# Column groups for a small projection, a later norm and earlier last-block preparations in a one-core decoder layer

## The chip, the core and the metric

The kernel runs on one core of a Trainium2 chip. The metric is the device time of one execution in microseconds, lower is better. The kernel before takes 1133.27 us, the median of 3 runs from 1133.16 to 1133.73. The engines are named as the profile names them: PE (TensorE), DVE (VectorE), ACT (ScalarE), POOL (GpSimd) and SP (SyncE, which issues most DMAs).

## What is computed

One decoder layer over 1088 tokens: a prompt of 1024 and 8 samples of 8 tokens. Three token mixers share one input projection; then comes a squared-ReLU MLP of width 4096. All is float32.

```python
h = rmsnorm(x, g1)
proj = h @ w_in            # 2816 columns of mixers A, B, C, and 8 columns dt_raw
...
dt = jax.nn.softplus(dt_raw + dt_bias)
y, ssm_new = ssd(xs, dt, A, Bm, Cm, ssm_prev)
yc = rmsnorm(y * jax.nn.silu(z), ssm_norm)
x = x + jnp.concatenate([ya, yb, yc], axis=-1) @ w_out
f = jnp.square(jax.nn.relu(rmsnorm(x, g2) @ w_ff1))
x = x + f @ w_ff2          # then the final norm
```

The norm of a token is a factor `rstd` that multiplies its projected columns afterwards, so the projections can start before it is known. `dt_raw` has only 8 columns.

## The kernel before

Tokens lie along the free axis, features along 128 partitions; x is 8 tiles (`xts[k]`) of 128 x 1088. Products are made from float32 pairs: every operand is split into a rounded high part and the rest (low part), in float32r, and a product is hi·hi + lo·hi + hi·lo, in three chunks of 364, 364 and 360 tokens (`CH`).

**Start.** The loop over k (from line 240) makes for each tile the high part of x times g1 (line 248 on DVE for the first three, line 246 on ACT for the others), the low part (line 251, DVE), the square of the tile before, in place (`square`, line 234, ACT), and from the fourth tile on adds a square to the sum `ss` (`add_square`, line 238, DVE). `w_split` casts a weight tile to its high part on ACT (line 100) and subtracts on DVE (line 101). The first gemm group (lines 327 to 338) runs over k and makes the first projection (lines 330 and 334) and the 8 dt columns (line 337): the dt weights are split in place into a tile of 32 columns (8 high, 8 low, 16 zeros, lines 203 to 207 and 254), so that one product with the high and one with the low part of x does, into 32 partitions, in three chunks. The second projection is a `gemm` over chunks (lines 131 to 133); after its first chunk stands `rms_scale` (line 172 on PE, then lines 173 to 183 on ACT and DVE), which makes `rstd` out of `ss`. Its chunks are evacuated times `rstd` (line 286), the first projection and dt are multiplied afterwards (lines 351 and 353), and `conv_c` follows for both: a start on ACT (line 300), three multiply-adds each on DVE (line 303), a SiLU (line 305), and small copies of the buffer's edges on POOL (lines 296 and 297). The buffers `cb` are two, so the third projection is evacuated into one that a `conv_c` has released. PSUM slots for the projections (`gp`) are three. `dt_tokens` (lines 373 and 375) turns dt to tokens by partition, by products between the chunks of the third projection.

**Last block.** The MLP goes in 8 blocks; in each, `ff1` and `ff2` make their products by seven weight combinations of four quarters (11, 12, 21, 22) of a weight block. `wsums` makes sums of quarters (lines 989 to 991), `prep` splits a combination (line 101, or line 908 into `wl` tiles for two of the last), `load_q` loads a quarter of the next half-block on SP (line 979), `operand` splits an activation form (lines 907 to 911; forms by line 937, which also adds products into x). In the last block `ff1` has products `pos` 0 to 6 in the order (1, 2, 6, 7, 5, 3, 4), and `ff2_last` goes through a list of units (position, row tile), each 12 products of 272 columns. A product group takes a PSUM bank; line 1189 is an ACT copy that frees two of them.

The order on each engine is fixed when the program is built. It follows the order of the code, but what is ready goes ahead of what is not; the tail from `last_products` on is in an order written out by hand. Each engine works its queue strictly in that order.

Of the kernel before, what the change touches and what calls it, by code (L numbers as in the profile page):

```python
# [15 lines left out]
P = 128  # L16
D = 1024
# [54 lines left out]
def body(nc, tc, I, O):  # L72
# [130 lines left out]
    wdt = sml.tile([P, KT, 32], F32R, name="wdt")  # L203
    wd = C("wdt").rearrange("p (k m) -> p k m", m=8)
    zz = sml.tile([P, KT, 16], F32, name="zz")
    G.memset(zz, 0.0)
    V.tensor_copy(out=wdt[:, :, 16:32], in_=zz)
# [31 lines left out]

    for k in range(KT):  # L240
        xt = xts[k]
        b = big[:, k * 2 * T:(k + 1) * 2 * T].rearrange("p (h t) -> p h t", h=2)
        g = C("g1")[:, k:k + 1]
        for a, e in (((0, 364), (364, T)) if k == 0 else ((0, T),)):
            if k > 2:
                S.activation(out=b[:, 0, a:e], in_=xt[:, a:e], func=AF.Identity, scale=g)
            else:
                V.tensor_scalar(out=b[:, 0, a:e], in0=xt[:, a:e], scalar1=g, scalar2=None, op0=ALU.mult)
        if k == 0:
            w_split(0)  # L250
        V.scalar_tensor_tensor(out=b[:, 1], in0=xt[:, :T], scalar=g, in1=b[:, 0].bitcast(F32),
                               op0=ALU.mult, op1=ALU.subtract)
        if k == 0:
            V.tensor_copy(out=wdt[:, :, 0:8], in_=wd)
            V.tensor_tensor(out=wdt[:, :, 8:16], in0=wd, in1=wdt[:, :, 0:8].bitcast(F32),
                            op=ALU.subtract)
        if k:
            square(k - 1)
        if k > 2:
            add_square(k - 2)  # L260
        xg.append(b)
    w_split(1)
    square(KT - 1)
    add_square(KT - 2)
    add_square(KT - 1)
# [59 lines left out]
    psd = [ap.tile([P, 512], F32, name="aps", tag="a") for _ in CH]  # L325
    w0 = next_w()
    for k in range(KT):
        for h in range(2):
            for ps, (c0, n) in zip(ps0, CH):
                PE.matmul(ps[:, :n], w0[:, 0, k * P:(k + 1) * P], xg[k][:, h, c0:c0 + n],  # L330
                          start=k == 0 and h == 0, stop=k == KT - 1 and h == 1)
            if h == 0:
                for ps, (c0, n) in zip(ps0, CH):
                    PE.matmul(ps[:, :n], w0[:, 1, k * P:(k + 1) * P], xg[k][:, 0, c0:c0 + n],
                              start=False, stop=False)
            for ps, (c0, n) in zip(psd, CH):
                PE.matmul(ps[:32, :n], wdt[:, k], xg[k][:, h, c0:c0 + n],  # L337
                          start=k == 0 and h == 0, stop=k == KT - 1 and h == 1)
# [4 lines left out]
    dtT = tmpp.tile([P, T], F32, name="dtT", tag="t")[:32]  # L343
    for ps, (c0, n) in zip(psd, CH):
        S.copy(out=dtT[:, c0:c0 + n], in_=ps[:32, :n])
    buf5 = new_buf(3, C("sst")[:, 5 * 24:6 * 24])
    gemm(next_w(), xg, range(KT), lambda c, ps: evac_pad(c, ps, buf5, 3),
         first=ap.tile([P, 512], F32, name="aps", tag="a"), hooks=[lambda: rms_scale(aslots(), catp, "yb", ss, rstd, D, False)])
# [4 lines left out]
    V.tensor_tensor(out=dtT, in0=dtT, in1=rstd[:32], op=ALU.mult)  # L353
# [13 lines left out]
    def dt_tokens(cs):  # L367
        if not dpv:
            dps = ap.tile([P, 512], F32, name="aps", tag="a")
            dpv.append(dps[:, :72].rearrange("p (c h) -> p c h", h=8))  # L370
        for c in cs:
            if c < NC:
                PE.matmul(dpv[0][:, c], dtT[:, c * L:(c + 1) * L], C("eye2")[:32], start=True, stop=True)
            else:
                PE.matmul(dpv[0][:TS, NC], dtT[:, SEQ:T], C("eye2")[:32], start=True, stop=True)
# [605 lines left out]
    def wsums(hb):  # L981
        if (hb, "s1") in raw:
            return
        a11, a21, a22 = (raw[hb, q] for q in ("11", "21", "22"))
        s1 = raw[hb, "s1"] = wrp.tile([P, 1024], F32, name="ws", tag="wr")
        raw[hb, "s2"] = a11
        if hb == 0:
            raw[hb, "s2"] = qtile("ws")[:, :1024]
        V.tensor_tensor(out=s1, in0=a21, in1=a22, op=ALU.add)
        V.tensor_tensor(out=a21, in0=a21, in1=a11, op=ALU.add)  # L990
        V.tensor_tensor(out=raw[hb, "s2"], in0=a11, in1=s1, op=ALU.add)
# [7 lines left out]
    def prep(n):  # L999
# [20 lines left out]
        if pos == 3:  # L1020
            load_q(hb + 1, "11")
            load_q(hb + 1, "21")
        if j == 4:
            load_q(hb + 1, "22")
        elif j == (6 if 0 < hb < 2 * NFB - 1 else 3):
            wsum4(hb)
            load_q(hb + 1, "12")
# [66 lines left out]
    def ff1(i):  # L1094
# [31 lines left out]
        for pos, j in enumerate(ords):  # L1126
# [33 lines left out]
            elif j == 6:  # L1160
                if i:
                    copy_out("12", ps)
                else:
# [9 lines left out]
            elif j == 3:  # L1173
                if i:
                    add_in("12", ps)
                    relu2("12", 1.0)
                    if i == NFB - 1:
                        operand(i, f, 0)
# [22 lines left out]
            if i == NFB - 1:  # L1201
                if pos == 4:
                    f["op22"] = fviews(x % 3 * XS)
                    split_f(f["op22"], f["22"], slice(0, NH), 1.0)
                elif pos == 5:
                    wsums(2 * NFB - 1)
                    prep(LAST2 + 4)
                elif pos == 6:
                    prep(LAST2 + 3)
# [27 lines left out]
    def ff2_operand(f, j, dst):  # L1237
        src = form(j, f["11"], f["12"], f.get("21"), f["22"], op)
# [64 lines left out]
    def ff2_last(f):  # L1303
# [15 lines left out]
        units = [(0, 0), (0, 1), (0, 2), (1, 0), (0, 3), (1, 1), (2, 0), (1, 2), (2, 1), (1, 3), (3, 0), (2, 2),  # L1319
# [281 lines left out]
```

## Time and profile before

| | |
|---|---|
| median of 3 runs | 1133.27 us |
| profiled execution, its own time | 1133.37 us |
| its span, first to last instruction | 1131.6 us |
| PE busy | 1118.3 us |
| DVE busy | 836.4 us |
| ACT busy | 498.3 us |
| POOL busy | 62.3 us |
| granted PE clock, mean | 0.997 of full |

Busy time is the union of an engine's instruction times. Matmuls are pipelined and their ends are modelled, so the distance between two starts says more than a duration. An idle engine costs something only where the chain that ended last passes through it.

### The profile page before, as it was taken

The numbers are of one execution on the slowest core, as the hardware profiler recorded it, in microseconds if no ns is written. First come the engines' busy times: TensorE is split into PE (matmuls) and PEld (weight loads), VectorE is DVE, ScalarE is ACT, GpSimd is POOL, SyncE is SP. The second block draws the span as 40 slices with busy tenths as digits, with TensorE's granted clock in tenths as the row PEclk, the third lists the DMA queues.
The fourth block names the chain that finished last, engine by engine and source line by source line (L and its number), as shares of the span: only waits on it lengthen the run. The fifth ranks groups of instructions, "written<-read, shape, count | busy, mean of one in ns | idle before, by whom it ended". The sixth has DMA issues, their size and how long they took to land.

```text
span 1131.6 us, 19854 instructions
## 1 busy us (share of the span) xinstructions
PE 1118.3 (99%) x8482; PEld 1099.0 (97%) x8482; DVE 836.4 (74%) x1108; ACT 498.3 (44%) x660; POOL 62.3 (6%) x94
## 2 busy tenths in 40 slices
PE   8999999999999999999999999999999999999996
PEld 6999999999999999999999999999999999999996
DVE  8875587965655476989697497497596596599596
ACT  6545273423553334753342442443443442533544
POOL 1410021110000000000000000000000000000016
PEclk9999999999999999999999999999999999999998
DMA  6112233321137253692853953953953943954404
GB/s 258 52 50 69 60 113 104 113 69 53 34 99 272 84 223 123 281 394 79 311 197 114 391 198 131 387 187 142 384 190 140 385 182 152 376 175 159 195 1 159
DMA packets 34776, 200.43 MB, mean 177 GB/s; under 512 B 4736, under 2 KB 7680, under 8 KB 27776
## 3 DMA queue, kind: packets, MB, share of 16 engines
q1 hardware_dynamic: 32592, 196.30, 46.8%
q10 hardware_dynamic: 2096, 2.85, 0.7%
q8 instruction: 67, 1.10, 0.4%
q14 instruction: 21, 0.17, 0.0%
HBM read 175.58 MB, written 22.77 MB: 175 GB/s over the span
## 4 chain that ended last, share of the span: by engine, by line
PE 94%; DVE 4%; DMA 1%; issue 0%; ACT 0%; POOL 0%; SPq 0%; POOLq 0%; ACTq 0%
PE ps L1035 19%; PE ps L1034 19%; PE ps L1036 18%; PE gps L131 10%; PE gps L132 10%; PE gps L133 10%; PE aps L565 1%; DVE x L937 1%; PE aps L569 1%; DVE whl L101 1%; DMA xt<-xT 1%; PE gps L330 1%; PE aps L337 0%; DVE xq L902 0%; DVE big L908 0%
## 5 line engine op out<-in xcount | busy, mean ns | idle before, releaser
L1034 PE MATMUL ps<-big,whl 128*128 128x272 f32 x1312 | 377.6, 288 | 0.2 <-DVE f L1116 0.2
L1035 PE MATMUL ps<-big,whl 128*128 128x272 f32 x1312 | 377.6, 288 | 0.0
L1036 PE MATMUL ps<-big,whl 128*128 128x272 f32 x1312 | 376.9, 287 | 0.0
L1034 PEld LDWEIGHTS ps<-big,whl 128*128 128x128 f32 x1312 | 247.1, 188 | 0.6 <-DVE f L1116 0.5
L1035 PEld LDWEIGHTS ps<-big,whl 128*128 128x128 f32 x1312 | 247.1, 188 | 0.0
L1036 PEld LDWEIGHTS ps<-big,whl 128*128 128x128 f32 x1312 | 246.8, 188 | 0.0
L131 PE MATMUL gps<-big,whl 128*128 128x360 f32 (+2 forms) x752 | 240.0, 319 | 0.0
L132 PE MATMUL gps<-big,whl 128*128 128x360 f32 (+2 forms) x752 | 236.6, 315 | 0.3 <-DVE whl L101 0.3
L133 PE MATMUL gps<-big,whl 128*128 128x360 f32 (+2 forms) x752 | 236.0, 314 | 0.0
L100 ACT CAST whl<-wq 128x1024 fp32r<-128x1024 f32 x92 | 96.5, 1051 | 226.7 <-PE ps L1036 131.3
L101 DVE TENSOR_TENSOR whl<-wq,whl 128x1024 fp32r<-128x1024 f32 x92 | 112.5, 1222 | 55.8 <-ACT whl L100 55.6
L131 PEld LDWEIGHTS gps<-big,whl 128*128 128x128 f32 x752 | 141.5, 188 | 0.9 <-ACT big L778 0.2
L132 PEld LDWEIGHTS gps<-big,whl 128*128 128x128 f32 x752 | 141.4, 188 | 0.9 <-DVE whl L101 0.5
L133 PEld LDWEIGHTS gps<-big,whl 128*128 128x128 f32 x752 | 141.3, 188 | 0.0
L937 DVE TENSOR_TENSOR x<-x,ps 128x544 f32<-128x544 f32 x188 | 130.6, 716 | 6.7 <-PE ps L1036 5.7
L1036 PE MATMUL ps<-fo,whl 128*128 128x272 f32 x416 | 119.6, 288 | 0.2 <-DVE fo L911 0.2
L1035 PE MATMUL ps<-fo,whl 128*128 128x272 f32 x416 | 119.3, 287 | 0.3 <-DVE whl L101 0.3
L1034 PE MATMUL ps<-fo,whl 128*128 128x272 f32 x416 | 119.4, 287 | 0.0
L100 ACT CAST whl<-wst 128x1024 fp32r<-128x1024 f32 (+2 forms) x39 | 40.0, 1026 | 133.2 <-PE gps L133 84.2
L1036 PEld LDWEIGHTS ps<-fo,whl 128*128 128x128 f32 x416 | 78.2, 188 | 0.7 <-DVE fo L911 0.7
L1035 PEld LDWEIGHTS ps<-fo,whl 128*128 128x128 f32 x416 | 78.2, 188 | 0.5 <-DVE whl L101 0.5
L1034 PEld LDWEIGHTS ps<-fo,whl 128*128 128x128 f32 x416 | 78.4, 188 | 0.1
(325 smaller groups left out, 1406.1 us busy)
## 6 DMA issues: line engine op xcount, KB each, us to landing
big<-xcd SPq DMA_DIRECT2D x47, 2176.0 KB, 9.9
wq<-w SPq DMA_DIRECT2D x66, 512.0 KB, 4.5
xcd<-big SPq DMA_DIRECT2D x7, 2176.0 KB, 8.6
wst<-w_in SPq DMA_DIRECT2D x21, 512.0 KB, 3.6
wst<-w_out SPq DMA_DIRECT2D x16, 512.0 KB, 3.6
x<-xT SPq DMA_DIRECT2D x8, 544.0 KB, 5.4
dec<-scr SPq DMA_DIRECT2D x8, 512.0 KB, 3.8
xt<-xT SPq DMA_DIRECT2D x7, 544.0 KB, 8.8
```

Of the source, the lines that this page charges most:

```text
L100: S.copy(out=w[:, 0, a:b], in_=st[:, a:b])
L101: V.tensor_tensor(out=w[:, 1, a:b], in0=st[:, a:b], in1=w[:, 0, a:b].bitcast(F32), op=ALU.subtract)
L131: PE.matmul(ps[:, :n], hi, xh, start=start, stop=False)
L132: PE.matmul(ps[:, :n], lo, xh, start=False, stop=False)
L133: PE.matmul(ps[:, :n], hi, xl, start=False, stop=stop)
L330: PE.matmul(ps[:, :n], w0[:, 0, k * P:(k + 1) * P], xg[k][:, h, c0:c0 + n], start=k == 0 and h == 0, stop=k == KT - 1 and h == 1)
L565: PE.matmul(yps[hh * HD:(hh + 1) * HD, i * L:(i + 1) * L], w[:, h * HD:(h + 1) * HD], m[:, h], start=i == 0 and n == 0, stop=n == len(term ...
L569: PE.matmul(sps[:, g * 256:(g + 1) * 256], bt[:, g * P:(g + 1) * P], xw[:, g * 256:(g + 1) * 256], start=True, stop=True)
L937: V.tensor_tensor(out=out, in0=a, in1=b, op=o)
L1034: PE.matmul(o, hi, xh, start=start and k == 0, stop=False, skip_group_check=True)
L1035: PE.matmul(o, lo, xh, start=False, stop=False, skip_group_check=True)
L1036: PE.matmul(o, hi, xl, start=False, stop=k == ks - 1, skip_group_check=True)
```

## The change

In the start: the dt weights are multiplied by g1 once and kept in plain float32, with 24 columns of zeros behind the 8. `dt_products(k)` multiplies them with the raw tile `xts[k]` as soon as it is loaded, in four groups of 256 prompt tokens, each into its own 32 partitions of one PSUM tile, and two groups of 32 sample tokens beside them. These stand in the code ahead of each tile's split; the 48 dt products in the first gemm group go. All additions of squares stand behind the loop and the second weight split. The norm (`rms_scale`) stands after the second chunk of the second projection instead of the first, and the first chunk's evacuation is held until then. dt is multiplied by `rstd` in six pieces, before the first projection is, and `dt_tokens` reads it from four partition groups, with one more product.

In the last block: for the last half-block quarter 22 is loaded before 12 instead of after it; `wsums` is made in two parts, the first two sums after `pos` 3; the split of combination 4 (`LAST2 + 3`) stands after `pos` 4 instead of 6; the first operand's split stands two products earlier; and in `ff2_last` unit (0, 3) stands before (1, 0).

```diff
@@ -200 @@
-    wdt = sml.tile([P, KT, 32], F32R, name="wdt")
-    wd = C("wdt").rearrange("p (k m) -> p k m", m=8)
-    zz = sml.tile([P, KT, 16], F32, name="zz")
-    G.memset(zz, 0.0)
-    V.tensor_copy(out=wdt[:, :, 16:32], in_=zz)
+    wdt = sml.tile([P, KT, 32], F32, name="wdt")
+    G.memset(wdt, 0.0)
@@ -237 @@
+    V.tensor_tensor(out=wdt[:, :, 0:8], in0=C("wdt").rearrange("p (k m) -> p k m", m=8),
+                    in1=C("g1").unsqueeze(2).broadcast_to([P, KT, 8]), op=ALU.mult)
+    psd = ap.tile([P, 512], F32, name="aps", tag="a")
+    DTQ = SEQ // 4
+
+    def dt_products(k):
+        parts = [(j, 0, DTQ, j * DTQ) for j in range(4)] + [(j, DTQ, 32, SEQ + 32 * j) for j in range(2)]
+        for j, o, n, t in parts:
+            PE.matmul(psd[32 * j:32 * j + 32, o:o + n], wdt[:, k], xts[k][:, t:t + n],
+                      start=k == 0 and o == 0, stop=k == KT - 1, skip_group_check=True)
+
     for k in range(KT):
         xt = xts[k]
+        dt_products(k)
...
-        if k == 0:
-            V.tensor_copy(out=wdt[:, :, 0:8], in_=wd)
-            V.tensor_tensor(out=wdt[:, :, 8:16], in0=wd, in1=wdt[:, :, 0:8].bitcast(F32),
-                            op=ALU.subtract)
         if k:
             square(k - 1)
-        if k > 2:
-            add_square(k - 2)
         xg.append(b)
     w_split(1)
     square(KT - 1)
-    add_square(KT - 2)
-    add_square(KT - 1)
+    for k in range(KT):
+        add_square(k)
@@ -333 @@
-            for ps, (c0, n) in zip(psd, CH):
-                PE.matmul(ps[:32, :n], wdt[:, k], xg[k][:, h, c0:c0 + n],
-                          start=k == 0 and h == 0, stop=k == KT - 1 and h == 1)
...
-    dtT = tmpp.tile([P, T], F32, name="dtT", tag="t")[:32]
-    for ps, (c0, n) in zip(psd, CH):
-        S.copy(out=dtT[:, c0:c0 + n], in_=ps[:32, :n])
+    dtT = tmpp.tile([P, T], F32, name="dtT", tag="t")[:, :DTQ + 32]
+    S.copy(out=dtT[:, :DTQ], in_=psd[:, :DTQ])
+    S.copy(out=dtT[:64, DTQ:], in_=psd[:64, DTQ:DTQ + 32])
...
-    gemm(next_w(), xg, range(KT), lambda c, ps: evac_pad(c, ps, buf5, 3),
-         first=ap.tile([P, 512], F32, name="aps", tag="a"), hooks=[lambda: rms_scale(aslots(), catp, "yb", ss, rstd, D, False)])
+    held = []
+
+    def evac_late(c, ps):
+        held.append((c, ps))
+        while c and held:
+            evac_pad(*held.pop(0), buf5, 3)
+
+    gemm(next_w(), xg, range(KT), evac_late, first=ap.tile([P, 512], F32, name="aps", tag="a"),
+         hooks=[lambda: None, lambda: rms_scale(aslots(), catp, "yb", ss, rstd, D, False)])
+    for j in range(4):
+        r = slice(32 * j, 32 * j + 32)
+        V.tensor_tensor(out=dtT[r, :DTQ], in0=dtT[r, :DTQ], in1=rstd[r, j * DTQ:(j + 1) * DTQ], op=ALU.mult)
+        if j < 2:
+            V.tensor_tensor(out=dtT[r, DTQ:], in0=dtT[r, DTQ:], in1=rstd[r, SEQ + 32 * j:SEQ + 32 * j + 32],
+                            op=ALU.mult)
...
-    V.tensor_tensor(out=dtT, in0=dtT, in1=rstd[:32], op=ALU.mult)
@@ -1020 @@
+        first, second = ("22", "12") if hb == 2 * NFB - 2 else ("12", "22")
         if j == 4:
-            load_q(hb + 1, "22")
+            load_q(hb + 1, second)
         elif j == (6 if 0 < hb < 2 * NFB - 1 else 3):
             wsum4(hb)
-            load_q(hb + 1, "12")
+            load_q(hb + 1, first)
@@ -1160 @@
                 if i:
                     copy_out("12", ps)
+                    if i == NFB - 1:
+                        operand(i, f, 0)
...
                     if i == NFB - 1:
-                        operand(i, f, 0)
                         operand(i, f, 1)
@@ -1202 @@
                 if pos == 4:
                     f["op22"] = fviews(x % 3 * XS)
                     split_f(f["op22"], f["22"], slice(0, NH), 1.0)
+                    prep(LAST2 + 3)
+                elif pos == 3:
+                    wsums(2 * NFB - 1, False)
                 elif pos == 5:
                     wsums(2 * NFB - 1)
                     prep(LAST2 + 4)
-                elif pos == 6:
-                    prep(LAST2 + 3)
@@ -1316 @@
-        units = [(0, 0), (0, 1), (0, 2), (1, 0), (0, 3), (1, 1), (2, 0), (1, 2), (2, 1), (1, 3), (3, 0), (2, 2),
+        units = [(0, 0), (0, 1), (0, 2), (0, 3), (1, 0), (1, 1), (2, 0), (1, 2), (2, 1), (1, 3), (3, 0), (2, 2),
```

## Rows read from the trace of the kernel before

**Rows 1.** The page, part 1: busy time, share of the span, instructions.

```profile
PE 1118.3 (99%) x8482; PEld 1099.0 (97%) x8482; DVE 836.4 (74%) x1108; ACT 498.3 (44%) x660; POOL 62.3 (6%) x94
```

**Rows 2.** Table by stretches: stretch; us, busy per engine (instructions); PEclk, DMA, GB/s.

```profile
38.00:56.00 18.00, 18.00 (x112) 17.23 (x111) 17.63 (x25) 7.79 (x7) 11.60 (x10) 1.00 0.10 30
60.00:1050.00 990.00, 989.46 (x7563) 979.21 (x7562) 726.49 (x949) 420.83 (x549) 24.50 (x48) 1.00 0.50 185
1075.50:1097.00 21.50, 21.50 (x174) 21.50 (x174) 21.50 (x27) 8.16 (x11) 0.00 (x0) 1.00 0.01 2
```

**Rows 3.** Timeline of PE, start: start, length, instruction, count, [idle before <-releaser].

```profile
4.49 0.77 PE L337 MATMUL aps<-big,wdt 128*32 128x364 f32 x1
...
27.53 0.33 PE L131 MATMUL aps<-big,whl 128*128 128x364 f32 x1
...
31.52 1.99 PE L172 MATMUL aps<-ss,cp 128*128 128x364 f32 x6
...
55.98 0.43 PE L131 MATMUL gps<-big,whl 128*128 128x364 f32 x1
```

**Rows 4.** Chain that ended last: start, length to the next step, what.

```profile
31.68 1.83 PE aps L172 x6
...
56.05 0.36 PE gps L131
56.42 0.17 PE gps L132
...
158.82 1.90 PE aps L565 x32
```

**Rows 5.** Timeline of ACT, 11 to 25 us: high parts, squares, weight cast.

```profile
11.50 2.50 ACT L246 ACTIVATE big<-xt,cp 128x1088 fp32r<-128x1088 f32 x2 [0.40 <-DMA xt<-xT]
...
20.57 2.20 ACT L234 ACTIVATE xt<-xt 128x1088 f32<-128x1088 f32 x2
22.67 1.03 ACT L100 CAST whl<-wst 128x1024 fp32r<-128x1024 f32 x1
```

**Rows 6.** Timeline of DVE, 3 to 57 us.

```profile
11.42 1.28 DVE L238 TENSOR_TENSOR ss<-ss,xt 128x1088 f32<-128x1088 f32 x1
...
22.75 1.34 DVE L251 SCALAR_TENSOR_TENSOR big<-xt,cp,big 128x1088 fp32r<-128x1088 f32 x1
...
25.22 1.21 DVE L101 TENSOR_TENSOR whl<-wst,whl 128x1024 fp32r<-128x1024 f32 x1
...
27.67 1.29 DVE L238 TENSOR_TENSOR ss<-ss,xt 128x1088 f32<-128x1088 f32 x1
...
36.57 0.99 DVE L180 TENSOR_TENSOR rt<-rstd 128x364 f32<-128x364 f32 x2 [1.89 <-ACT rstd L177]
...
43.39 1.27 DVE L353 TENSOR_TENSOR dtT<-dtT,rstd 32x1088 f32<-32x1088 f32 x1
44.59 1.21 DVE L101 TENSOR_TENSOR whl<-wst,whl 128x1024 fp32r<-128x1024 f32 x1
45.73 7.79 DVE L303 SCALAR_TENSOR_TENSOR xc<-cb,cp,xc 128x1112 f32<-128x1112 f32 x6
53.89 0.98 DVE L286 TENSOR_TENSOR cb<-gps,rstd 128x364 f32<-128x364 f32 x2 [0.37 <-POOL stC L297]
```

**Rows 7.** Timeline of POOL, 42 to 54 us.

```profile
43.28 10.29 POOL L296 COPY stC<-cb 128x3 f32<-128x3 f32 x1 [0.19 <-DVE cb L286]
```

**Rows 8.** Timeline of PE, last block.

```profile
1073.08 0.29 PE L1036 MATMUL ps<-big,whl 128*128 128x272 f32 x1
...
1075.47 0.29 PE L1034 MATMUL ps<-fo,whl 128*128 128x272 f32 x1
...
1097.10 0.29 PE L1036 MATMUL ps<-big,wl 128*128 128x272 f32 x1
...
1097.84 0.29 PE L1035 MATMUL ps<-big,wl 128*128 128x272 f32 x1
```

**Rows 9.** Timeline of ACT, last block.

```profile
1070.67 2.00 ACT L100 CAST whl<-wq 128x1024 fp32r<-128x1024 f32 x2 [3.23 <-PE ps L1036]
...
1074.61 1.13 ACT L1189 ACTIVATE f<-ps 128x544 f32<-128x544 f32 x2
```

**Rows 10.** Timeline of DVE, last block.

```profile
1065.06 1.22 DVE L989 TENSOR_TENSOR ws<-wq 128x1024 f32<-128x1024 f32 x1
...
1075.11 1.22 DVE L908 TENSOR_TENSOR wl<-wq,wl 128x1024 fp32r<-128x1024 f32 x1
```

**Rows 11.** DMA view, 1055 to 1057 us: issue, count, KB each, median us to landing.

```profile
wq<-w SPq DMA_DIRECT2D x1, 512.0 KB, 7.8
```

More of the change, by code (lines that the diff above doesn't have):

```diff
@@ L324, in body @@
     ps0 = [gp.tile([P, 512], F32, name="gps", tag="g") for _ in CH]
-    psd = [ap.tile([P, 512], F32, name="aps", tag="a") for _ in CH]
     w0 = next_w()
@@ L372, in dt_tokens @@
             if c < NC:
-                PE.matmul(dpv[0][:, c], dtT[:, c * L:(c + 1) * L], C("eye2")[:32], start=True, stop=True)
-            else:
-                PE.matmul(dpv[0][:TS, NC], dtT[:, SEQ:T], C("eye2")[:32], start=True, stop=True)
+                o = 32 * (c // 2)
+                PE.matmul(dpv[0][:, c], dtT[:, c % 2 * L:(c % 2 + 1) * L], C("ident")[:, o:o + 8],
+                          start=True, stop=True)
+            else:
+                for j in range(2):
+                    o = 32 * j
+                    PE.matmul(dpv[0][o:o + 32, NC], dtT[:64, DTQ:], C("ident")[:64, o:o + 8], start=True, stop=True)
     def softplus():
@@ L979, in load_q, with wsums @@
             SY.dma_start(out=t, in_=I["w1" if hb % 2 == 0 else "w2"][hb // 2, QS[q]])
-    def wsums(hb):
-        if (hb, "s1") in raw:
+    def wsums(hb, s2=True):
+        a11, a21, a22 = (raw[hb, q] for q in ("11", "21", "22"))
+        if (hb, "s1") not in raw:
+            s1 = raw[hb, "s1"] = wrp.tile([P, 1024], F32, name="ws", tag="wr")
+            V.tensor_tensor(out=s1, in0=a21, in1=a22, op=ALU.add)
+            V.tensor_tensor(out=a21, in0=a21, in1=a11, op=ALU.add)
+        if not s2 or (hb, "s2") in raw:
             return
-        a11, a21, a22 = (raw[hb, q] for q in ("11", "21", "22"))
-        s1 = raw[hb, "s1"] = wrp.tile([P, 1024], F32, name="ws", tag="wr")
+        s1 = raw[hb, "s1"]
         raw[hb, "s2"] = a11
@@ L988, in wsums @@
             raw[hb, "s2"] = qtile("ws")[:, :1024]
-        V.tensor_tensor(out=s1, in0=a21, in1=a22, op=ALU.add)
-        V.tensor_tensor(out=a21, in0=a21, in1=a11, op=ALU.add)
         V.tensor_tensor(out=raw[hb, "s2"], in0=a11, in1=s1, op=ALU.add)
@@ L1237, in ff2_operand @@
     def ff2_operand(f, j, dst):
-        src = form(j, f["11"], f["12"], f.get("21"), f["22"], op)
+        src = form(j, *(f.get(q) for q in ("11", "12", "21", "22")), op)
         split_f(dst, src, slice(0, NH), -1.0 if j == 6 else 1.0)
```

## The prediction

> **What bounds the kernel now.** I read the page's table of engines first, then the table by stretches, then TensorE's timeline and the chain of waits at both ends of the span. TensorE is busy nearly all of the span [rows 1], and from 60 to 1050 us without a break [rows 2], so in that middle nothing that another engine does faster can show: the change can gain only where TensorE does less or waits. It touches two such places. The first is the start: the first gemm group runs from 4.49 us to the next projection's first product at 27.53, the norm's products come at 31.52, and the fourth projection starts at 55.98 [rows 3]. The second is the last block, where VectorE is busy for every one of 21.5 us (1075.5 to 1097, [rows 2]) and TensorE's starts fall behind.
>
> **Start, TensorE's work.** Removed: 48 products of 32 columns by 360 or 364. A product of that width takes 0.166 us (31.52 − 27.53 is 24 of them [rows 3]), so 8.0 us. Left of the first group: 72 products, 12.0 us. Added, for each of 8 input tiles: four float32 products of 256 tokens in four column groups and two of 32. Float32 costs two passes each: six passes of about 363 columns take 1.83 us, 0.84 ns a column, so 0.215 us for a pass of 256 [rows 4]. Eight of these and four short ones (at 0.059 us, the shortest float32 pass in a row here) are 1.96 us one after the other. The trace has no four column groups; the nearest are the scan's products, in two groups of 64 columns: 32 passes of 128 columns in 1.90 us [rows 4], 0.059 each where 0.84 ns a column gives 0.107, so 1.8 times faster than one by one. Four groups that overlap alike give 1.96/3.6 = 0.54 us; in pairs only, 1.09; not at all, 1.96. The first product after a float32 burst takes 0.36 instead of 0.17 us [rows 4], 0.19 more. So 0.73 us an input tile, 5.8 us in all; bounds 10.2 (pairs) and 17.2 (none). I take 5.8: two groups do overlap almost fully, and four are the same thing again. The Trainium skill (TensorE: Matmul & The Clock Gate, "Measured speedup vs the span model") measured 2.38 times for three column tiles. With that factor for these four it would be 8.1 us, an estimate; no run here shows it yet, and it is weighed as a rival.
>
> TensorE then has 5.1 + 12.0 + 5.8 = 22.9 us plus its waits for inputs. Before, these waits are 23.0 − 120 × 0.166 = 3.1 us; with work to fill them I take 2: about 24.9.
>
> **Start, what the inputs allow.** This is the tighter end. ScalarE makes the high parts of the last five input tiles, the squares, and then the high part of the second weight tile; from 11.50 until that cast ends at 23.70 it has no idle time that counts [rows 5]. The change takes nothing off it there. Low parts that come sooner make squares ready sooner, and by the code's order a ready square goes ahead of the next high part: so the last high part (now 20.57, where the next squares start [rows 5]) gets no earlier, and the last low part, now 22.75 to 24.09 [rows 6], ends at 22 to 24.4. The second weight tile's cast still ends at 23.7, and its low part takes VectorE 1.21 us [rows 6]: 24.9 at best, 26.2 if a 1.28 us sum has just begun. Such sums do get in: the one at 11.42 ran ahead of a low part that stands before it in the code [rows 6]. Middle 25.5; the first product needs no low part, so the second projection starts at **25.4** instead of 27.53.
>
> The sums themselves lose nothing: VectorE is all but gapless from 3.4 us to the last sum's end at 28.96 [rows 6], its work is the same, and the norm now needs them only at 25.4 + 8.0 = 33.4. Removed with them: a cast and a subtraction for the small weights, a fill of zeros; added one product of 64 columns ahead of the first input's landing. Nothing of that is on the path.
>
> **Start, the norm a chunk later.** Here the change pays. The norm's products came 4.0 us after the second projection's start, now 8.0: 33.4 instead of 31.52, though that projection starts sooner. From there the chain is fixed: 5.05 us to the first multiplication of the correction at 36.57, then VectorE without a pause to 53.52 (17.6 of the 18 us from 38 to 56 [rows 2]; corrections, evacuations, dt, the weight split, six convolution steps of 1.3 us) [rows 6], 16.95 us. To this comes dt: one multiplication of 1.20 us becomes four of 256 and two of 32 tokens, at 1.20/1088 = 1.1 ns a column and, for the short ones, some 0.13 (an estimate): 1.5 us, 0.3 more. Then 0.37 us for GpSimd and 0.49 for the first evacuation of the third projection [rows 6], whose PSUM slot the fourth projection's first chunk needs (there are three). So the fourth projection can start 23.2 us after the norm's products: 33.4 + 23.2 = **56.6**. TensorE alone would be there at 25.4 + 28.45 + 0.2 = 54.1 (28.45 is 55.98 − 27.53; 0.2 the added token products). It waits 2.5 us, and the stage ends **0.6 us later** than before. What TensorE saved (2.2 us) is lost in VectorE's queue; break-even is a start of 24.8 for the second projection. Who waits behind that: the evacuations, in VectorE's queue behind the convolutions, and TensorE behind them. The dt token products, which wait for the multiplied dt in that queue, fall into the same wait.
>
> Could the evacuation slip in ahead of the last convolution step, 1.3 us sooner? Its target buffer is free only when GpSimd has copied the old one's edge, and this copy of 3 columns took 10.29 us, from VectorE's burst to its end [rows 7]. So I keep 23.2 and use 21.9 for the low end. The Trainium skill states the mechanism (SBUF — State Buffer, "Who interferes with whom"): the two engines share a port pair held for a whole instruction, and a VectorE operation with two SBUF inputs blocks GpSimd's reads. By that rule the copy can't pass the convolutions, and 56.6 stands; the trace agrees, with 10.29 us.
>
> **Last block.** TensorE's starts lie 0.125 us apart there; from 1073.08 to 1075.47 seven starts take 2.39 us, 1.5 more, and from 1097.10 to 1097.84 two take 0.74, 0.5 more [rows 8]. So **2.0 us** is all there is to gain. The first is the operand and weights of the second product group; the product group of the first weights that could fill it lacked a PSUM bank until ScalarE's copy at 1074.61 [rows 9]. That copy stood in ScalarE's queue behind a weight cast that waited 3.23 us for TensorE [rows 9]. The change puts two preparations (2 casts of 1.0 us on ScalarE, 2 subtractions of 1.22 on VectorE, the first now at 1075.11) and two weight sums of 1.22, the first at 1065.06 [rows 10], earlier, into idle time: 4.9 us less for VectorE in the stretch in which it is full. They can go there since the quarter that the sums need is now loaded first; the other lands 7.8 us after its issue at about 1055 [rows 11], 1063, ahead of its cast. The loads themselves are as many as before, on the same queue and slots. The fourth unit of the first weights now precedes the second weights' first: 1.5 us of work across the stall. Moving the first operand's split does nothing: its input is done long before. I take 1.7 of the 2.0; low bound 0.3, if the waiting cast stays at the head of ScalarE's queue.
>
> **Sum.** +0.6 − 1.7 = −1.1 us against the profiled execution's 1133.37 (span 1131.6, so 1.8 lies around it), which is 0.1 over the median of 1133.27; set against the median, as the times below: **1132.2**. A measurement of this kernel can tell about 0.2% from no change, 2.3 us; so this is "the same".
>
> **Rivals.**
> - Input pacing is better than I think. If ScalarE's program takes the weight cast ahead of two squares (1.1 us each), the second projection starts at 23.7 (TensorE-bound with 0.8 us of waits). The norm's chain then ends at 54.9, −1.1; with all 2.0 of the last block 1130.2, and with the evacuation one step sooner 1128.9. For it: the weights have long landed. Against: the order seen before [rows 5].
> - Slower: the column groups do not overlap. Then 17.2 us of products; the second projection starts at 5.1 + 12.0 + 17.2 = 34.3, the fourth at 65.5, +9.5, and the time is 1141.1. It decides from 28.8 us for the second projection's start on (11.7 us of dt products, 1.46 a tile), which is about where pairs are: 5.1 + 12.0 + 10.2 + 1.0 = 28.3, +3.5, and with 0.5 of the last block 1136.3. Against it: the two-group row.
> - The groups overlap by halves: 2.4 times, between the 1.8 of two groups and 3.6. Then 1.96/2.4 + 0.19 = 1.01 us a tile, 8.1 in all, the second projection starts at 5.1 + 12.0 + 8.1 + 2 = 27.2, 1.8 later than forecast, and the time is 1134.0. The skill's 2.38 cited above is this case; the two-group row speaks for more.
> - The change does not do what it says in the last block: the cast still blocks ScalarE, gain 0.3: 1133.6.
>
> **How the numbers follow.** My forecast 0.42, the better pacing 0.28, no overlap or pairs 0.12, overlap by halves 0.09, the unchanged last block 0.09. The better pacing is faster, no overlap and pairs are slower, the other three are "same" but for 0.02 of the forecast on the fast side: faster 0.30, same 0.58, slower 0.12. The range goes from 1128.9 to 1136.3, the better pacing's low end and the pairs'.
>
> **What would show it.** The second projection's first product at 25.4 (24.8 to 26.2); the gap between dt products of one tile (0.54 us a tile, or near 1.1, or 1.96); the norm's products after 33 us; a TensorE wait of 2 to 3 us before the fourth projection, released by VectorE's evacuation; starts 0.125 us apart around 1073. A start under 24, no wait at 54 to 57, or the norm's products ahead of the second chunk would make the first half wrong; a stall of over 1 us at the second weights' first product the other.

## The result and the profile after

The changed kernel takes 1136.19 us, the median of 9 runs (1133.98 to 1137.43). The kernel before, run beside it, takes 1133.27 us (9 runs, 1132.67 to 1134.03). The ratio is 1.0022 with a 95% interval of 1.0012 to 1.0031: slower, by a small amount that the interval sets apart from no change. Forecast were 1132.2 and "the same". The measured time lies just inside the upper edge of the range, and the sign is wrong. Of the experiments' runs below, two took about twice as long as the rest (2210.34 us with the norm at the first chunk, 2318.74 us with the last block alone); the ratios leave them out.

The profiled execution of the changed kernel took 1137.18 us (span 1135.1), 3.8 more than the profiled one of the kernel before; the spans differ by 3.5. It is one of the longer of the nine, so what is read from it explains more than the 2.9 us by which the medians differ. That the runs of the changed kernel spread over 3.4 us, those of the kernel before over 1.4, is a first hint.

The page's table of engines, which answers to [rows 1]:

```profile
PE 1119.1 (99%) x8532; PEld 1099.2 (97%) x8532; DVE 837.2 (74%) x1111; ACT 497.5 (44%) x659; POOL 54.0 (5%) x94
```

By its totals nothing happened, except that POOL does 8 us less. Such a table can't show a loss of 4 us in the start. TensorE's waits there can: the view of waits, PE from 4 to 70 us, its two longest (engine and tile that waited, engine that released it; us in total, times, longest). The longest one in the kernel before is 0.65 us in that window.

```profile
PE gps L131 <- DVE cb L291: 3.4, 1, 3.4
PE aps L387 <- DVE dtT L359: 1.2, 1, 1.2
```

And TensorE's timeline, which answers to [rows 3] (start, length, instruction, count, idle time before and who ended it):

```profile
19.24 0.66 PE L334 MATMUL gps<-big,whl 128*128 128x364 f32 x3
19.83 0.69 PE L247 MATMUL aps<-xt,wdt 128*32 128x256 f32 x12
20.45 0.77 PE L334 MATMUL gps<-big,whl 128*128 128x364 f32 x3
21.05 0.66 PE L338 MATMUL gps<-big,whl 128*128 128x364 f32 x3
...
25.05 0.33 PE L131 MATMUL aps<-big,whl 128*128 128x364 f32 x1
25.66 0.79 PE L131 MATMUL gps<-big,whl 128*128 128x364 f32 x2 [0.29 <-ACT cb L343]
26.96 0.43 PE L132 MATMUL aps<-big,whl 128*128 128x364 f32 x1 [0.50 <-DVE whl L101]
...
34.70 1.99 PE L172 MATMUL aps<-ss,cp 128*128 128x364 f32 x6
47.17 0.84 PE L387 MATMUL aps<-cp,dtT 128*128 128x8 f32 x6 [1.21 <-DVE dtT L359]
...
59.30 0.64 PE L131 MATMUL gps<-big,whl 128*128 128x364 f32 x1 [3.44 <-DVE cb L291]
...
89.79 0.33 PE L437 MATMUL aps<-av,cp 128*128 128x64 f32 x2
```

The second projection begins 2.5 us sooner than before (25.05 against 27.53), the norm's products (L172) come 3.2 later (34.70 against 31.52), and the fourth projection 3.3 later (59.30 against 55.98). The last row is a product some thirty microseconds on, the first of the running sums; in the kernel before the same product is this row:

```profile
84.04 0.33 PE L420 MATMUL aps<-av,cp 128*128 128x64 f32 x2
```

From the fourth projection to it TensorE took 28.06 us before (84.04 − 55.98) and 30.49 after (89.79 − 59.30), 2.43 us more for the same products, without any wait in between. The table by stretches says why (stretch; its length, busy us and instructions of PE, PEld, DVE, ACT, POOL; granted clock, DMA share, GB/s):

```profile
5.50:57.90 52.40, 48.17 (x338) 41.99 (x336) 44.20 (x57) 30.50 (x37) 4.79 (x8) 1.00 0.39 148
57.90:64.70 6.80, 5.40 (x18) 5.43 (x19) 6.39 (x11) 6.34 (x7) 2.86 (x7) 0.50 0.27 80
```

TensorE stopped at 55.86; 2 us later the granted clock fell to 0.50, the lower of its two levels (1.2 GHz of 2.4), and stayed there until 64.7, over the first 5.4 us of the fourth projection. The kernel before has no such stretch between 5.6 and 1120 us; its granted clock is 1.00 in all three stretches of [rows 2]. So the start lost 3.3 us because the fourth projection stands later, and 2.4 by the clock. VectorE's queue, which answers to [rows 6]:

```profile
23.09 2.68 DVE L236 TENSOR_TENSOR ss<-ss,xt 128x1088 f32<-128x1088 f32 x2
25.69 1.22 DVE L101 TENSOR_TENSOR whl<-wst,whl 128x1024 fp32r<-128x1024 f32 x1
...
39.75 0.99 DVE L180 TENSOR_TENSOR rt<-rstd 128x364 f32<-128x364 f32 x2 [1.89 <-ACT rstd L177]
...
44.66 0.41 DVE L359 TENSOR_TENSOR dtT<-dtT,rstd 32x256 f32<-32x256 f32 x1
45.00 0.58 DVE L291 TENSOR_TENSOR cb<-gps,rstd 128x296 f32<-128x296 f32 x2
45.50 0.17 DVE L361 TENSOR_TENSOR dtT<-dtT,rstd 32x32 f32<-32x32 f32 x1
...
46.27 0.85 DVE L359 TENSOR_TENSOR dtT<-dtT,rstd 32x256 f32<-32x256 f32 x2
47.15 1.50 DVE L365 TENSOR_TENSOR cb<-cb,rstd 128x364 f32<-128x364 f32 x4
48.56 1.22 DVE L101 TENSOR_TENSOR whl<-wst,whl 128x1024 fp32r<-128x1024 f32 x1
49.70 1.29 DVE L468 TENSOR_TENSOR ss<-rstd 128x1088 f32<-128x1088 f32 x1
50.90 7.81 DVE L308 SCALAR_TENSOR_TENSOR xc<-cb,cp,xc 128x1112 f32<-128x1112 f32 x6
58.62 0.98 DVE L291 TENSOR_TENSOR cb<-gps,rstd 128x364 f32<-128x364 f32 x2
```

It has no gap from 39.75 to the evacuation at 58.62 that TensorE waits for (the copy of finished sums out of PSUM, which frees their slot). One row is new in that place: L468, the square of `rstd` for a later mixer, 1.29 us. In the kernel before it stood behind the evacuation:

```profile
53.89 0.98 DVE L286 TENSOR_TENSOR cb<-gps,rstd 128x364 f32<-128x364 f32 x2 [0.37 <-POOL stC L297]
54.79 1.34 DVE L451 TENSOR_TENSOR ss<-rstd 128x1088 f32<-128x1088 f32 x1
```

In the last block the two stalls of [rows 8] are all but gone. These starts stand where the long stall was; about 0.3 us are lost there instead of 1.5:

```profile
1078.79 0.29 PE L1056 MATMUL ps<-big,whl 128*128 128x272 f32 x1
1079.09 0.36 PE L1054 MATMUL ps<-fo,whl 128*128 128x272 f32 x1
1079.29 0.29 PE L1055 MATMUL ps<-fo,whl 128*128 128x272 f32 x1
```

From 84 to 1071 us TensorE stays 5.7 us behind the kernel before; at 1120 it is 3.9 behind. So the account of the profiled run up to there is 3.3 + 2.4 − 1.8 = 3.9; at the end of the spans it is 3.5, and 0.3 of the 3.8 lies outside them.

### The profile page after: what moved, and what is told of

The parts are those of the page before. It is cut to its first block, busy times and chain, and to the rows that moved or that the text cites. A ratio compares the mean times of both kernels' runs of the same rounds, so it can differ in the third digit from the quotient of the medians.

```text
span 1135.1 us, 19966 instructions
## 1 busy us (share of the span) xinstructions
PE 1119.1 (99%) x8532; PEld 1099.2 (97%) x8532; DVE 837.2 (74%) x1111; ACT 497.5 (44%) x659; POOL 54.0 (5%) x94
## 4 chain that ended last, share of the span: by engine, by line
PE 93%; DVE 3%; issue 1%; DMA 1%; ACT 0%; POOL 0%; SPq 0%; POOLq 0%; DVEq 0%; ACTq 0%
PE ps L1054 19%; PE ps L1055 19%; PE ps L1056 19%; PE gps L131 10%; PE gps L132 10%; PE gps L133 9%; PE aps L582 1%; DMA xt<-xT 1%; PE aps L586 1%; DVE big L262 1%; DVE xc L308 1%; DVE xq L919 0%; DVE whl L101 0%; PE p L1054 0%; PE aps L517 0%
```

## Experiments

Theory A: the later norm lengthens VectorE's chain until TensorE waits for its end, and that wait costs more than itself, since the clock falls behind it. Rivals: the column groups, the sums or the last block lose the time; or the wait costs itself only.

**Each part alone.** First the changed kernel with the norm back at the first chunk, everything else kept:

```diff
-    gemm(next_w(), xg, range(KT), evac_late, first=...,
-         hooks=[lambda: None, lambda: rms_scale(...)])
+    gemm(next_w(), xg, range(KT), lambda c, ps: evac_pad(c, ps, buf5, 3), first=...,
+         hooks=[lambda: rms_scale(...)])
```

> The changed kernel with one part undone: the norm stands after the first chunk of the second projection again, and its chunks are evacuated without being held. Theory A (the later norm delays VectorE's queue, TensorE waits 3.4 us for it before the fourth projection, and its clock falls after that wait): the norm's products come at about 31 us, VectorE's convolutions end at about 55, the fourth projection starts at about 55.4 with no wait over 0.5 us, no stretch at half clock before the end, and the time is about 1131 us (0.6 us from the start, 1.8 from the last block, against 1133.3). Theory B (the loss comes from the dt column groups and the input stage, whatever the norm does): still about 1136 us, with a start that is 3 us or more behind at 84 us.

Measured: 1130.63 us, ratio to before 0.9975 (0.9966 to 0.9985). The norm's products come at 30.32, the fourth projection at 55.01, and there is no stretch at half clock:

```profile
55.01 0.41 PE L131 MATMUL gps<-big,whl 128*128 128x364 f32 x1 [1.30 <-DVE cb L291]
...
83.04 0.33 PE L437 MATMUL aps<-av,cp 128*128 128x64 f32 x2
```

28.03 us lie between these two, as before. The wait of 1.3 us is more than the 0.5 expected at most. Everything but the norm's place gains 3 us; the norm's place, on top of the rest, costs 5.6 (1136.19 − 1130.63).

The opposite, the kernel before with only the norm a chunk later and the first chunk's evacuation held (the same lines the other way round):

> The kernel before with one part of the change alone: the norm a chunk later (and the first chunk's evacuation held). Theory A: the norm's products move from 31.5 to 35.5 us, the fourth projection waits for VectorE until about 58.4 instead of 55.98, and the time is 1135.7 us, or up to 1138 when the clock falls in the wait. Theory B: TensorE is covered by the work in its queue, and the time stays at 1133.3 us.

Measured: 1137.68 us, ratio 1.0036 (1.0023 to 1.0048). The fourth projection comes at 59.01 after a wait of 1.6 us (and 0.9 for dt before), and the clock is at 0.50 from 58.8 to 62.1. So this part loses with or without the others, 4.1 us by itself (1137.68 − 1133.60) and 5.6 on top of them.

The last block's part alone, on the kernel before:

```diff
+        first, second = ("22", "12") if hb == 2 * NFB - 2 else ("12", "22")
...
+                    prep(LAST2 + 3)
+                elif pos == 3:
+                    wsums(2 * NFB - 1, False)
...
+        units = [(0, 0), (0, 1), (0, 2), (0, 3), (1, 0), ...
```

> The kernel before with the last-block part of the change alone. The trace of the changed kernel shows the distance to the kernel before falling from 5.7 to 3.9 us between 1071 and 1120 us. If that is this part's own gain: 1.8 us faster, about 1131.5, with the stall at 1073 us gone. If it is only slack that the delay of the start left behind (loads landing earlier in relation to the work): no change, about 1133.3.

Measured: 1131.70 us beside 1133.60, ratio 0.9984 (0.9975 to 0.9993): 1.9 us of the 2.0 that [rows 8] allow.

The input part alone (column groups, sums behind the low parts), norm at the first chunk, last block as before:

```diff
+        dt_products(k)
...
-            for ps, (c0, n) in zip(psd, CH):
-                PE.matmul(ps[:32, :n], wdt[:, k], xg[k][:, h, c0:c0 + n], ...)
```

> The kernel before with the dt column groups and the sums behind the low parts alone: norm at the first chunk, last block as before. Theory A (the parts add up): what the run with the norm at the first chunk gained over the kernel before, 2.9 us, less the 1.9 of the last block alone, is about 1.0, so 1132.5 beside 1133.4 for the kernel before; a fourth projection at about 55.0 instead of 55.98. Rival B: without the last block's new order the start's gain doesn't reach the end, 1133.4.

Measured: 1132.29 us beside 1133.32, ratio 0.9992 (0.9983 to 1.0000): 1.0 us, and 1.0 + 1.9 is what the run with both gained. These two parts add up; the norm's place does not add to them (4.1 by itself, 5.6 on top). That the gain is not zero rests on a small margin by itself; the sum with the last block supports it. The profiled run, at 1133.01, doesn't show it: the fourth projection comes at 56.12 there, not at 55.0, behind a stretch at half clock from 8.3 to 11.7 us.

The sums' place, on the kernel with the norm at the first chunk:

```diff
+        if k > 2:
+            add_square(k - 2)
...
-    for k in range(KT):
-        add_square(k)
+    add_square(KT - 2)
+    add_square(KT - 1)
```

> The kernel with the norm back at the first chunk and the sums of squares where they were in the kernel before, between the low parts, instead of behind all of them. Theory A (the sums' place costs and gains nothing, since VectorE's work is the same and they fill its waits either way): 1130.6, the second projection's weights' low part at the same time or one sum (1.3 us) later. Rival B (sums ahead of the second weights' low part hold the second projection up by 1.3 us, and with it the norm's chain): 1131.9.

Measured: 1130.17 us, ratio 0.9973 (0.9962 to 0.9983), the same as with the sums behind (0.9975). The second weights' low part begins at 25.10 with a sum right ahead of it; with the sums behind, it begins at 25.11, and a sum stands ahead of it too. What is ready goes first, so on VectorE the place in the code hardly moved the sums. What a sum ahead of that low part costs, the run can't tell.

**The chain's length.** The square of `rstd` on ScalarE instead of VectorE, in the changed kernel:

```diff
-    V.tensor_tensor(out=ss, in0=rstd, in1=rstd, op=ALU.mult)
+    S.activation(out=ss, in_=rstd, func=AF.Square)
```

> The changed kernel with one instruction moved: the square of rstd (1.29 us, on VectorE at 49.7 us, ahead of the six convolution steps) is done by ScalarE. Theory A (the loss is VectorE's chain from the norm to the evacuation that TensorE waits for, plus the clock that falls behind the wait): the chain is 1.3 us shorter, TensorE's wait ahead of the fourth projection is about 2.1 us instead of 3.4, and that projection starts at about 58.0 instead of 59.3. If the clock still falls to 0.5 behind it for as long (cost 2.4 us), the time is 1136.2 - 1.3 = 1134.9; if it no longer falls, 1132.5. Rival B (the later norm costs time in another place, for instance by the PSUM banks that it holds longer, and the wait only shows it): the wait moves to another place and the time stays at 1136.

Measured: 1134.19 us, ratio 1.0009 (1.0000 to 1.0017), 2.0 less than the changed kernel. VectorE's rows:

```profile
48.10 1.22 DVE L101 TENSOR_TENSOR whl<-wst,whl 128x1024 fp32r<-128x1024 f32 x1
49.63 7.81 DVE L308 SCALAR_TENSOR_TENSOR xc<-cb,cp,xc 128x1112 f32<-128x1112 f32 x6 [0.31 <-ACT xc L305]
57.36 0.97 DVE L291 TENSOR_TENSOR cb<-gps,rstd 128x364 f32<-128x364 f32 x2
```

They show how the square came into the path: the first convolution step has to wait 0.31 us for ScalarE's start of it, the square was ready, and what is ready goes ahead of what isn't. An operation of 1.29 us filled a hole of 0.31. So the chain from the norm's products (34.24) to the fourth projection (58.04) is 23.8 us instead of 24.6, 0.8 shorter and not 1.3; that 58.04 agrees with the 58.0 expected is luck in part, since the norm's products came 0.46 us sooner in this profile. The wait is 1.0, and the clock fell all the same, but in another place, behind the 1.2 us that TensorE waited for dt:

```profile
48.40:51.70 3.30, 3.30 (x14) 3.30 (x12) 2.99 (x3) 2.41 (x2) 1.11 (x2) 0.50 0.41 99
```

There the slower products ended in the wait that was coming anyway, which is why the wait is 1.0 and not 2.1. The runs of this kernel spread from 1132.92 to 1136.72.

The same edit with the norm at the first chunk:

> The changed kernel with the norm back at the first chunk and the square of rstd on ScalarE. Theory A: the 1.3 us that TensorE waited ahead of the fourth projection at the first chunk's norm was the 1.29 us of that square in VectorE's queue; without it the projection starts at about 53.8 and the time is 1130.6 - 1.2 = 1129.4. Rival B: ScalarE's queue has no room there (silu and copies), or another wait takes its place, and the time stays at 1130.6.

Measured: 1129.87 us, ratio 0.9969 (0.9958 to 0.9981). The wait ahead of the fourth projection is 0.5 us, and that projection starts at 54.37, 0.64 sooner than without the edit, not 1.2. TensorE, there at 53.9, still waits for VectorE, whose evacuation comes 0.65 sooner (53.70 instead of 54.35): the hole of 0.31 us is there again, the chain is 0.8 shorter (23.90 from the norm's products instead of 24.69), and the norm's products stand 0.15 later. This is the best of the kernels run: 3.45 us under the kernel before, 6.3 under the changed one.

The second projection's convolution behind the third's evacuation:

```diff
-    conv_c(5, buf5)
...
         gemm(next_w(), xg, range(KT), lambda c, ps: evac_pad(c, ps, buf, 3), hooks)
+        if i == 6:
+            conv_c(5, buf5)
```

> The changed kernel, norm a chunk later, with the second projection's convolution (three of the six steps, 3.9 us of VectorE) placed behind the evacuation of the third projection instead of ahead of it. Same work, other order. Theory A (chain and clock): the evacuation that TensorE waits for comes 3.9 us sooner, the wait of 3.4 us is gone, the fourth projection starts at about 56, the clock doesn't fall, and the time is 1136.2 - 3.4 - 2.4 = 1130.4; if the next projection's evacuation is late instead, up to 1132. Rival B (the later norm costs in another place, or the clock falls for another reason than the wait): 1133.8 or more, and a stretch at half clock all the same.

Measured: 1134.68 us, ratio 1.0019 (1.0009 to 1.0028). Both the time and the stretch at half clock are what rival B had said, but the run doesn't test it, since the edit didn't do what it was for: the wait became 2.3 us, not zero. VectorE's rows show that the order came out otherwise than meant:

```profile
55.64 0.23 DVE L399 TENSOR_TENSOR xb<-aps,cp 128x64 f32<-128x64 f32 x1 [1.15 <-PE aps L393]
55.78 1.37 DVE L308 SCALAR_TENSOR_TENSOR xc<-cb,cp,xc 128x1112 f32<-128x1112 f32 x1
57.07 0.15 DVE L400 TENSOR_TENSOR xb<-aps,cp 64x8 f32<-64x8 f32 x1
57.26 1.49 DVE L291 TENSOR_TENSOR cb<-gps,rstd 128x364 f32<-128x364 f32 x4
```

Two small additions that wait for TensorE's token products went ahead of the evacuation that TensorE was about to wait for, and one convolution step with them. The evacuation came 1.4 us sooner, not 3.9. It decides between neither theory but repeats the pattern: a wait of 2.3 us, then half clock from 57.7 to 61.0.

**The wait itself.** A first attempt put 20 products, into a PSUM tile that nobody reads, ahead of the fourth projection, to keep TensorE busy through the wait:

```diff
     def softplus():
         dt_tokens((6, 7, 8))
+        fps = ap.tile([P, 512], F32, name="aps", tag="a")
+        for q in range(20):
+            PE.matmul(fps[:, :364], ones, xg[q % KT][:, 0, :364], start=q == 0, stop=q == 19)
```

> The changed kernel with 20 products more (128 rows, 364 tokens, into a PSUM tile that nobody reads) between the third and the fourth projection, 3.3 us of work where TensorE waited 3.4 us. Theory A with the clock as a cost of its own: the fourth projection starts as late as in the changed kernel, 59.3 us, but no half-clock stretch follows, and the time is about 2.4 us less than the changed kernel's, about 1134. If the half-clock stretch costs nothing or has another cause: no better than the changed kernel, 1136 us or more.

Measured: 1135.89 us, ratio 1.0019 (1.0010 to 1.0028). The result is closer to the second expectation, but the run missed its aim. The clock did not fall behind the filled wait, but at 49.8, behind the wait for dt, so TensorE reached the filler late (57.93), and 3.4 us of filler then went past the wait's end and pushed the fourth projection to 61.37. It shows that the fall isn't tied to one wait; it measures no price.

Two better ones followed. The first takes both waits away and leaves the norm where the change puts it. The second projection's convolution does only its first step (three VectorE steps are left out), and the dt token products stand together:

```diff
-    conv_c(5, buf5)
+    conv_c(5, buf5, 1)
...
-    ... (6, [lambda: dt_tokens((0, 1, 2)), lambda: dt_tokens((3, 4, 5)), softplus])
+    ... (6, [lambda: None, lambda: dt_tokens((0, 1, 2, 3, 4, 5)), softplus])
```

> The changed kernel with what TensorE waits for behind the norm taken away: the second projection's convolution does only its first step (its three VectorE steps, 3.9 us, are left out, so those channels come out other than the reference's), and the dt token products stand together at the end of the third projection, so none waits for the multiplied dt. The norm stays a chunk later. Theory A (the loss is the waits, and the clock that falls behind them): the waits of 1.2 and 3.4 us are gone, the fourth projection starts at about 59.3 - 4.6 = 54.7, no stretch at half clock between 10 and 1120 us, and the time is 1136.2 - 4.6 - 1 to 2 for the clock = 1129.6 to 1130.6. Rival B (the clock falls for another reason, such as the denser work since the column groups): a stretch at half clock all the same, and 1131.5 or more.

Measured: 1129.92 us, ratio 0.9968 (0.9957 to 0.9979). The norm's products come at 34.45, as late as in the changed kernel; the fourth projection at 54.13 without a wait, TensorE is busy for all of the stretch in which the changed kernel ran at half clock, and the clock stays (table by stretches):

```profile
57.00:66.00 9.00, 9.00 (x56) 9.00 (x55) 7.55 (x18) 4.97 (x5) 1.18 (x6) 1.00 0.19 59
```

The second puts a wait in where there was little: the kernel with the norm at the first chunk, whose correction now computes each square of `rstd` three times over (`rep` is 3 in this norm, 1 in the others):

```diff
+            for q in range(rep):
-            V.tensor_tensor(out=t[:, cs], in0=dst[:, cs], in1=dst[:, cs], op=ALU.mult)
+                V.tensor_tensor(out=t[:, cs], in0=dst[:, cs], in1=dst[:, cs], op=ALU.mult)
...
-    ... (6, [lambda: dt_tokens((0, 1, 2)), lambda: dt_tokens((3, 4, 5)), softplus])
+    ... (6, [lambda: None, lambda: dt_tokens((0, 1, 2, 3, 4, 5)), softplus])
```

> The opposite: the kernel with the norm back at the first chunk (1130.6 us, no stretch at half clock, a wait of 1.3 us ahead of the fourth projection) with a wait put in: the norm's correction computes its squares three times over, 6 operations of 0.45 us more on VectorE, 2.7 us more in the chain; the dt token products stand at the end of the third projection, so the wait is in one place. TensorE's work is the same. Theory A (a wait of that size costs itself and a clock fall behind it): a wait of about 4.0 us, the fourth projection at about 57.7, a stretch at half clock from about there on, and 1130.6 + 2.7 + 1.7 to 2.7 = 1135.0 to 1136.0. Rival B (a wait costs itself only): 1133.3, and the clock stays.

Measured: 1135.30 us, ratio 1.0017 (1.0009 to 1.0026), 4.7 more than without the wait, where a wait that costs only itself gives 2.7. TensorE's timeline and the table by stretches:

```profile
57.84 0.64 PE L131 MATMUL gps<-big,whl 128*128 128x364 f32 x1 [4.12 <-DVE cb L292]
...
87.28 0.33 PE L438 MATMUL aps<-av,cp 128*128 128x64 f32 x2
```

```profile
5.50:57.50 52.00, 47.35 (x338) 42.16 (x330) 47.88 (x64) 31.60 (x38) 5.80 (x10) 1.00 0.40 148
57.60:60.90 3.30, 3.06 (x10) 3.10 (x11) 2.99 (x8) 2.98 (x4) 1.76 (x5) 0.50 0.02 5
```

The fourth projection comes 2.83 us later than without the wait, and from there to the running sums TensorE takes 29.44 us instead of 28.03: 1.41 for the clock. Together 4.24, against 4.1 by which the spans differ. A long wait put into a kernel that is otherwise well brings the fall with it, and the waits taken away take it away. Theory A stands.

## Why the prediction was wrong

- **The dt products** were forecast at 0.73 us a tile, 0.54 for the products and 0.19 for the switch. The products take 0.62 (20.45 − 19.83), 3.2 times faster than one after the other, where I assumed 3.6. With the switch a tile costs 0.81: from 19.24 to 21.05 lie 1.81 us, and six products of 0.166 us make 1.00 of them. The Trainium skill's 2.38 times for three column tiles (TensorE: Matmul & The Clock Gate, "Measured speedup vs the span model") would have given 1.01 here, as in the rival of halves; the trace is faster. The slower rivals that I named (pairs, no overlap), and with them all my chance of "slower", are refuted.
- **The second projection's start** was forecast at 25.4 and is 25.05. TensorE was there without a wait, by its own work (forecast at 24.9), and not by the input's limit that I called the tighter end; so it was the wrong row to hang the sum on. "The first product needs no low part" is true, and the fourth one does: it waited until 26.96. With the 0.29 us that ScalarE's copy held up, 1.4 us were lost between the first product and the fourth. The low part ended at 26.9, past my latest case (26.2, one sum that has just begun): the cast ended at 24.05 and not 23.7, and behind the sum that was running VectorE did another one first.

```profile
23.02 1.03 ACT L100 CAST whl<-wst 128x1024 fp32r<-128x1024 f32 x1
```

- **The sums lose nothing**: right for their place in the code (the run with the sums woven in); that a sum runs ahead of the second weights' low part is a piece of the 1.4 us above.
- **The norm's products** were forecast at 33.4, eight microseconds after the start. They came at 34.70, by those 1.4 us, less the 0.35 by which the start was early, and one product (0.17) more ahead of them.
- **The chain** was forecast at 23.2 us and took 24.6 (59.30 − 34.70). Its first piece was exact (39.75 − 34.70 = 5.05). What failed is the sentence "from there the chain is fixed": I took VectorE's order over from the trace before. The square of `rstd`, behind the evacuation before, went ahead of it and takes 1.2 us of the chain (49.70 to 50.90); without it the chain is still 23.8 (the run with the square on ScalarE). The six dt pieces were sized at 1.5 us and take 2.0 (44.66 to 47.15, less the 0.5 of the evacuations in between), and from the evacuation's start to the product it is 0.68 us and not 0.49. GpSimd's 0.37 us fell away. The blocked copy of [rows 7] has no counterpart: its copies take 1.25 and 1.28 us, between 48.6 and 51.1. With the norm's place alone changed, both old pieces stay, the square behind the evacuation and a blocked copy (11.13 us), and there the chain is the 23.2 of the forecast (59.01 − 35.83). So it was the new order and the dt pieces, not the norm's place, that made it longer.
- **TensorE alone** was forecast to be there at 54.1. It was there at 55.9: the late products at 25 to 27 us (1.4) and a wait of 1.2 us for dt are more than the difference. That dt would be waited for I wrote off as falling "into the same wait"; it is a wait of its own, some 10 us ahead of the other.
- **The start's sum** was +0.6 and is +3.3: 1.3 for the norm, 1.4 for the chain. The wait that I forecast is there, with the releaser that I named, 3.4 us instead of 2.5.
- **The clock** is the term that was missing. I priced a TensorE wait at its own length. The rows of before couldn't show more, as TensorE has no wait over 0.65 us there; this was outside the trace, and I should have bounded it. It is 2.4 us in the profiled run, and where it falls, and for how long, differs between the kernels' profiles (3.4 us or 6.8). Whether that makes the spread of the times is not shown: the nine runs don't order by their mean granted clock (1135.39 us at 0.993, 1136.44 at 0.996).
- **The last block** was forecast at −1.7 of 2.0 and is −1.8 here, −1.9 by itself. Right, and at the two stalls named; which of its moves does it was not tested one by one.

So the direction failed on two terms: the chain and the norm together 2.7 us too short, and the clock, 2.4, not there at all. Either alone would have left the time within 0.2% of the kernel before: −1.1 + 2.7 is 1.6, −1.1 + 2.4 is 1.3.

What stays open: why the fall comes behind the first wait in some runs and behind the second in others. One profile a kernel can't tell. In the profile of the input part alone it came at 8.3 to 11.7 us, behind waits for the inputs, in a run 0.7 us over its median. Also not shown is what the changed kernel costs in a run without any fall. Its shortest, 1133.98, may be one, but its mean clock of 0.996 doesn't tell: the profiles with the wait put in (a fall) and without waits (none) both have it.

## What to carry to other kernels

A step that is put off in TensorE's order to give it more time moves the end of the chain behind it by the same amount; count that chain to the evacuation that the next PSUM slot needs, and count it in the new order, since every operation that is ready may slip into a hole much shorter than itself. A wait of some microseconds in dense TensorE work can cost more than its length (here 1.4 and 2.4 us more, behind 4.1 and 3.4 us): look at the granted clock behind each wait that a change creates. Measure, too, the parts of a change by themselves: here two gave 1.0 and 1.9 us, and the third took 4.1 by itself and 5.6 on top of them.

## What the runs showed of the hardware

The granted clock of TensorE fell to half within otherwise dense work behind waits as short as 1.2 us (the run with the square on ScalarE: wait until 46.7, 0.50 from 48.4 to 51.7, while TensorE was busy for all of that stretch), and behind 1.6, 2.3, 3.4 and 4.1 us in others; behind the one wait of 1.3 us in the kernel with the norm at the first chunk it did not, nor behind the same wait with the sums woven in or with the input part alone. The changed kernel and the runs with waits of 1.6 and 2.3 us had two waits, the first, for dt, of 0.9 to 1.2 us some ten microseconds ahead of the other; the run with 4.1 us had one. The fall cost 1.4 us where it covered 3.1 us of work and 2.4 where it covered 5.4, both read as the longer distance between the same two products. And float32 products of 32 columns in four column groups start 7 ns apart (19.833, 19.839, 19.846 and 19.853 us in the changed kernel's trace): eight passes of 256 columns and four short ones took 0.62 us, and 0.19 more went at their two ends.
